# Splitting one store of a gated linear unit: tile 1's output as two transfers by rows

## The chip, the cores and the metric

The kernel runs on one core of a Trainium2 chip. The time is the device time of one execution in microseconds (us); the time before is the median of three runs, and lower is better. One more execution was recorded by the hardware profiler; its own time stands beside its span below.

## The reference

The input has 8192 rows of 8192 float32. The left half of each row is multiplied by the sigmoid of the right half, so the output has 8192 rows of 4096 float32.

```python
def reference(x):
    a, b = np.split(x, 2, axis=-1)
    return a * (1 / (1 + np.exp(-b)))
```

The kernel reads 268.44 MB and writes 134.22 MB.

## The kernel before

**Tiles.** The rows are cut into 33 tiles. Tiles 1 to 31 have 256 rows, two on each of the 128 partitions; tiles 0 and 32 have 128 rows, one on each partition. The two rows of a partition are neighbours in memory, so a partition of a full tile loads 64 KiB in one piece (two rows of 32 KiB) and stores 32 KiB in one piece (two rows of 16 KiB). There are two input buffers (`x_sb0`, `x_sb1`) and two output buffers (`o_sb0`, `o_sb1`); tile i uses number i % 2 of both.

**Engines.** For every tile SyncE issues the load (L46), ScalarE overwrites the right halves with their sigmoid (L59), VectorE multiplies into the output buffer (L73), and ScalarE issues the store (L83) on its own DMA queue; only the two stores of the last tile are issued by SyncE. In the profile, q1 is SyncE's queue (all loads and the last tile's stores), and q10 is ScalarE's (all other stores). Both queues feed the same 16 DMA engines. A full tile is worked on in one piece of 8192 elements per partition; tiles 1 and 31 in four of 2048, tile 0 in three pieces and tile 32 in two.

**What waits for what.** No scheduler is at work: the order is the program's.

- The load of tile i+2 waits until the multiplications of tile i have ended (semaphore `product`, L49), since they free the input buffer.
- The first sigmoid of a tile waits for its load. In tile 1, whose two rows per partition are loaded by two transfers, the third sigmoid waits for the second transfer (`row`, L68).
- The first multiplication of tile i waits on `ready[s]` both for its sigmoid and for the landing of the store of tile i-2, which frees the output buffer. `stored[s]` counts what such a store adds to that semaphore: 16 for each transfer.
- The store of tile i waits for `product` to reach `done[i]`, the number of multiplications up to and with tile i. It stands on ScalarE's queue behind the sigmoids of tile i and ahead of those of tile i+1. Tile 0 makes three products and tile 1 four, so `done[0]` is 3 and `done[1]` is 7.

The main loop is:

```python
for i in range(n):
    self.work(i, works.get(i, whole))
    if i + SLOTS < n:
        self.load(i + SLOTS)
    if i == 0:
        self.store(0, 0, half // 2, 2)
        self.store(0, half // 2, half, 3)
    elif i < n - 1:
        self.store(i)
```

`close` (L114 to L124) ends the program: SyncE waits for the last tile's stores, GpSimd for the other stores, and then clears the semaphores.

Of the kernel before, what the change touches and what calls it, by code (L numbers as in the profile page):

```python
# [16 lines left out]
class _Program:  # L17
# [75 lines left out]
    def trace(self):  # L93
        n, half = self.n_tiles, self.half
        one = slice(0, 1)
        whole = [(slice(0, R), slice(0, half))]
        fourths = [(slice(r, r + 1), c) for r in range(R) for c in HALVES]
        works = {0: [(one, c) for c in (QUARTERS[0], QUARTERS[1], HALVES[1])], 1: fourths,
                 n - 2: fourths, n - 1: [(one, c) for c in HALVES]}
        self.load(1, slice(0, 1))  # L100
        self.load(1, slice(1, 2), self.row)
# [4 lines that stand above are left out]
            if i == 0:  # L106
                self.store(0, 0, half // 2, 2)
                self.store(0, half // 2, half, 3)
            elif i < n - 1:
                self.store(i)  # L110
        for k, c in enumerate(HALVES):
            self.store(n - 1, c.start, c.stop, self.products - 1 + k)
# [69 lines left out]
```

## Time and profile before

| | |
|---|---|
| median of three runs | 933.2 us (933.19 to 933.42) |
| the profiled execution's own time | 933.03 us |
| its span | 931.7 us |
| DMA, mean over the span | 432 GB/s |
| VectorE busy | 279.1 us (30%) |
| ScalarE busy | 227.4 us (24%) |
| share of the DMA engines' time, q1 and q10 | 67.2% and 32.8% |

The span runs from the first to the last recorded instruction; the execution's own time is 1.3 us longer. The digits under "busy tenths" are shares of 40 equal slices of the span. A DMA "share" is the time that packets took, divided by 16 engines and by the stretch. A packet is what one DMA engine moves in one piece; the trace has a record of each with its start, its length and its size. Since a transfer of 128 partitions is spread over 16 engines, each engine has 8 of its packets, and behind them a packet of 4 bytes that counts up the semaphore. TensorE is not used.

### The profile page before, as it was taken

The numbers are of one execution on the slowest core, as the hardware profiler recorded it, in microseconds if no ns is written. First come the engines' busy times: TensorE is split into PE (matmuls) and PEld (weight loads), VectorE is DVE, ScalarE is ACT, GpSimd is POOL, SyncE is SP. The second block draws the span as 40 slices with busy tenths as digits, with TensorE's granted clock in tenths as the row PEclk, the third lists the DMA queues.
The fourth block names the chain that finished last, engine by engine and source line by source line (L and its number), as shares of the span: only waits on it lengthen the run. The fifth ranks groups of instructions, "written<-read, shape, count | busy, mean of one in ns | idle before, by whom it ended". The sixth has DMA issues, their size and how long they took to land.

```text
span 931.7 us, 200 instructions
## 1 busy us (share of the span) xinstructions
DVE 279.1 (30%) x42; ACT 227.4 (24%) x43; POOL 0.2 (0%) x4
## 2 busy tenths in 40 slices
DVE  1312333113332133321333213332133321333233
ACT  2332033320333202332023330233302333023331
POOL 0000000000000000000000000000000000000000
DMA  9999999999999999999999999999999999999999
GB/s 400 450 411 450 425 430 428 450 428 428 428 445 456 405 442 435 429 450 419 459 405 430 447 428 450 428 450 405 428 450 448 430 411 461 411 450 428 426 429 405
DMA packets 9937, 402.67 MB, mean 432 GB/s; under 512 B 1104, under 2 KB 1104, under 8 KB 1104
## 3 DMA queue, kind: packets, MB, share of 16 engines
q1 hardware_dynamic: 5184, 270.53, 67.2%
q10 hardware_dynamic: 4752, 132.12, 32.8%
q14 instruction: 1, 0.01, 0.0%
HBM read 268.44 MB, written 134.22 MB: 432 GB/s over the span
## 4 chain that ended last, share of the span: by engine, by line
DMA 73%; DVE 15%; ACT 12%; DVEq 0%; issue 0%
DMA x_sb<-in_x_dram 73%; DVE o_sb L73 15%; ACT x_sb L59 12%; DVEq L117 0%
## 5 line engine op out<-in xcount | busy, mean ns | idle before, releaser
L73 DVE TENSOR_TENSOR o_sb<-x_sb 128x8192 f32<-128x8192 f32 (+2 forms) x42 | 279.1, 6659 | 646.9 <-ACT x_sb L59 646.9
L59 ACT ACTIVATE x_sb<-x_sb 128x8192 f32<-128x8192 f32 (+2 forms) x42 | 226.1, 5401 | 694.5 <-DMA x_sb<-in_x_dram 694.5
L59 ACT ACT_TABLE_LOAD x1 | 1.3, 1283 | 1.5 <-PEq L148 1.5
L166 POOL MEMSET const-bfloat16-1.0<- 128x1 bf16 x1 | 0.1, 101 | 0.0
L166 POOL MEMSET const-uint8-127<- 128x1 uint8 x1 | 0.1, 101 | 0.0
L166 POOL MEMSET const-float32-0.0<- 128x1 f32 x1 | 0.1, 98 | 0.2 <-issue 0.2
L166 POOL MEMSET const-float32-1.0<- 128x1 f32 x1 | 0.1, 98 | 0.0
## 6 DMA issues: line engine op xcount, KB each, us to landing
out_dram<-o_sb ACTq DMA_DIRECT2D x31, 4096.0 KB, 34.8
x_sb<-in_x_dram SPq DMA_DIRECT2D x4, 4096.0 KB, 26.9
out_dram<-o_sb ACTq DMA_DIRECT2D x2, 1024.0 KB, 24.6
out_dram<-o_sb SPq DMA_DIRECT2D x2, 1024.0 KB, 5.5
x_sb<-in_x_dram SPq DMA_DIRECT2D x30, 42.2
```

The source lines that it names most:

```text
L59: sig = nc.scalar.activation(out=b, in_=b, func=mybir.ActivationFunctionType.Sigmoid)
L73: mul = nc.vector.tensor_mul(out=packed[:, r, c], in0=rows[:, r, 0, c], in1=rows[:, r, 1, c])
L166: nc = _bacc.Bacc("TRN2", target_bir_lowering=False, num_devices=1)
```

## The change

Tile 1's store was one transfer: 128 pieces of 32 KiB, issued when all four products of the tile were done. Now it is two transfers. The first takes the first row of every partition (128 pieces of 16 KiB) and waits for two products of tile 1, the second takes the second row and waits for all four. Both are issued by ScalarE one behind the other, where the one store was, and each adds 16 to `ready[1]`, for which the first multiplication of tile 3 waits. Nothing else differs.

```diff
             if i == 0:
                 self.store(0, 0, half // 2, 2)
                 self.store(0, half // 2, half, 3)
+            elif i == 1:
+                self.store(1, 0, half, self.done[0] + 2)
+                self.store(1, half, 2 * half, self.done[1])
             elif i < n - 1:
                 self.store(i)
```

## The prediction

> **What bounds the kernel now.** I read the page first: the span, the DMA slices, the queues.
>
> ```profile
> span 931.7 us, 200 instructions
> ...
> DMA  9999999999999999999999999999999999999999
> ...
> DMA packets 9937, 402.67 MB, mean 432 GB/s; under 512 B 1104, under 2 KB 1104, under 8 KB 1104
> ...
> q1 hardware_dynamic: 5184, 270.53, 67.2%
> q10 hardware_dynamic: 4752, 132.12, 32.8%
> ```
>
> The DMA engines are busy in every slice, and the two queues' shares add up to the whole span. The 1104 small packets are semaphore writes, 16 for each of 69 transfers. Busy time by stretch confirms it (columns: stretch, length, DVE, ACT, POOL, clock, DMA share, GB/s):
>
> ```profile
> 59.00:88.00 29.00, 8.69 (x1) 7.12 (x2) 0.00 (x0) 1.00 1.00 434
> 88.00:117.00 29.00, 8.69 (x1) 6.94 (x1) 0.00 (x0) 1.00 1.00 434
> ```
>
> A full tile takes 29.0 us of DMA and 15.7 us of engine work. Next the waits: engines wait for loads, and nothing waits for a store.
>
> ```profile
> ACT x_sb L59 <- DMA x_sb<-in_x_dram: 694.5, 34, 22.4
> DVE o_sb L73 <- ACT x_sb L59: 646.9, 35, 24.7
> ```
>
> Then the timeline around tile 1 and at the end (start, length, what):
>
> ```profile
> 41.48 0.36 ACTq L83 DMA_DIRECT2D out_dram<-o_sb  x1
> 59.07 7.03 ACT L59 ACTIVATE x_sb<-x_sb 128x8192 f32<-128x8192 f32 x1 [20.35 <-DMA x_sb<-in_x_dram]
> ...
> 87.91 7.03 ACT L59 ACTIVATE x_sb<-x_sb 128x8192 f32<-128x8192 f32 x1 [21.81 <-DMA x_sb<-in_x_dram]
> 94.97 8.69 DVE L73 TENSOR_TENSOR o_sb<-x_sb 128x8192 f32<-128x8192 f32 x1 [20.15 <-ACT x_sb L59]
> ```
> ```profile
> 919.57 3.71 ACT L59 ACTIVATE x_sb<-x_sb 128x2048 f32<-128x2048 f32 x2 [12.05 <-DMA x_sb<-in_x_dram]
> 921.51 4.49 DVE L73 TENSOR_TENSOR o_sb<-x_sb 128x2048 f32<-128x2048 f32 x2 [10.46 <-ACT x_sb L59]
> 923.83 3.02 SPq L83 DMA_DIRECT2D out_dram<-o_sb  x2
> ```
>
> Store 1 is issued at 41.48. The packet records place its first packet at 53.3, since the second store of tile 0 holds the queue until 50.6 (first engine) to 51.0. They also show the rule between the queues: each DMA engine alternates packet by packet, whatever the sizes: 64 KiB load, 8 KiB store, 64 KiB load at 34 to 50 us; 64 KiB, 32 KiB, 64 KiB afterwards. A semaphore write takes a turn too. So a full tile is 9 turns on either side, and loads and stores stay in step. Median packet times: 64 KiB 2.418 us, 32 KiB 1.213, 8 KiB 0.309, semaphore write 0.009.
>
> So the end is set by the sum of packet times, as long as neither queue's lag leaves the DMA engines without work.
>
> **The change part by part.**
>
> *More packets.* From 8 and 32 KiB, a packet is 37.7 ns per KiB plus 7.7 ns; 16 KiB gives 0.610 us. Each DMA engine has 16 x 0.610 in place of 8 x 1.213, and one more semaphore write: 8 x 7.7 + 9 = 70 ns. Successive packets overlap by some 4 ns in the records, so the lower bound is 0.03 us. I take +0.07 us: it lies on the bound resource.
>
> *The earlier first half.* Its two products end at 29.3, but ScalarE gets to it only behind the fourth sigmoid, at 38.7, still 2.8 us before 41.48. The queue ahead is full until 50.6, so no byte moves earlier: 0. Its issue takes 0.36 us on ScalarE, which is idle until 59: 0 as well. No load is behind it: those are on SyncE.
>
> *The turn count.* This is the real effect. Store 1 now takes 18 turns (16 packets, 2 semaphore writes) in place of 9, and loads get a 64 KiB packet against each 16 KiB. Counting from 53.3: 16 half packets (9.8 us) and the 15 load packets between them (36.3) put the second half's semaphore write at 99.3, where the single store's came at 79.9. Load 3 gains in the same turns: its last packet ends near 81, ScalarE starts at about 81.6 (before: 87.91). Its multiplication could start at 88.6 but now waits for store 1 until 99.8: a new wait of 11 us, end 108.5 (before 103.7). Behind it on VectorE nothing is due; ScalarE stands at store 3, so sigmoid 4 waits as well; SyncE's load 5 waits.
>
> Does DMA run dry? At 99.3 load 4 still has two packets and store 2 all eight: 2 x 2.42 + 8 x 1.21 = 14.5 us of work, until 113.8. Load 5 and store 3 are issued at 108.5. From issue to first packet I have 1.9 us as the upper value (final store: 923.83 to 925.74) and 1.05 as the lower (first load). So the queues fill again at 110.4, 3.4 us before the work ends. The load queue is empty from about 106.5, but DMA writes store 2 meanwhile, at the same 1.213 per packet as stores alone have at 919 to 925. Cost: 0, cover 3.4 us.
>
> *Afterwards.* Both sides are again 9 turns a tile, so the shift stays: loads land about 5 us earlier than before (tile 5's sigmoid near 141 instead of 146), stores land later, about 49 us after issue (now 34.8), and a multiplication may wait some us for its output buffer. Load i+2 is still issued more than 10 us before load i+1 ends.
>
> *The tail.* Before, the final stores' first packet at 925.74 follows directly the last of store 31 (925.73): no gap, no margin. After, load 32 lands about 5 us earlier, the final stores queue at about 921 and share turns with store 31. Order changes, the sum doesn't: 0.
>
> **Sum:** 933.03 + 0.07 = 933.10 for the profiled execution. The median of the runs is 0.17 above that execution, so +0.07 gives 933.27; I say 933.3. Bounds of the small terms: three stalls of some 0.35 us on load packets (at 18.6, at 50.5 when store 1 comes up, and one engine delayed at 718 by an instruction fetch, so that it ended 0.3 us behind the rest) may each go or come again: -0.8 to +0.8.
>
> [...] Two rows stand for what a further transfer costs: tile 0's two stores follow each other on the queue with only a load packet between, no gap; a final store, mostly uncovered, takes 5.4 us from issue to landing, of which 8 x 0.309 = 2.5 is movement. [...]
>
> **Rivals.**
>
> 1. *DMA runs dry once (slower).* If the alternation favours loads more than turn for turn, load 4 is finished before store 1 lands. Then store 2's 8 x 1.213 = 9.7 us must cover multiplication 3: 0.5 of landing, 8.7 and 1.9 make 11.1. Gap 1.4 us, and the first packet after an idle stretch took some 1.85 instead of 1.21: +2.0 in all, 935.1. It decides when less than 11.1 us of work is queued at store 1's landing; I count 14.5. It comes once, since load 5 and store 3 then start together. For it: the new wait on the chain. Against: the packet records alternate strictly from 34 to 60, at three packet sizes. Chance 0.09.
> 2. *The further transfer's fixed cost is paid (slower).* At most 5.4 - 2.5 = 2.9 us: 936.0. Against it the gapless stores of tile 0. Chance 0.04.
> 3. *The slack helps (faster).* The earlier loads relieve the tail and stalls vanish: 0.8 off, 932.4, still within 0.2%. Chance 0.08. More would need fewer packet times, and there is no idle DMA time to win: 0.03.
> 4. *The split doesn't shift the queues* (two 16 KiB pieces count as one turn): no wait appears, 933.2, same verdict. Chance 0.06.
>
> **How the numbers follow.** The forecast gets the remaining 0.70. Within 0.2% (1.9 us, about what a measurement of this kernel can tell from no change) lie the forecast, rival 4 and the smaller case of rival 3: 0.84. Slower: rivals 1 and 2, 0.13. Faster: 0.03. The range goes from the small terms' low end, 932.4, to rival 1's 935.1.
>
> **What would show it.** Right: 10081 packets, 1120 of them small; q10 4896; DMA share 1.00 in every 29 us stretch; tile 3's sigmoid near 81.6 and its multiplication near 99.8, put down to a store; stores landing about 49 us after issue. Rival 1 would show a stretch near 110 to 115 with a DMA share under 1. I am wrong if the tail shows idle DMA, or if tiles take more than 29.0 us each.

## The result, and the profile after

The change makes the kernel slower, by just under one per cent. Over 22 runs of each kernel the median is 941.84 us after and 933.06 before; the ratio, which goes by the means, is 1.0078, 95% interval 1.006 to 1.0095. The runs after fall into two groups: five between 933.17 and 933.66, as forecast, and seventeen between 940.57 and 944.68. The profiled execution is of the second group: 942.08 us, span 940.8.

The page after, the lines that answer to those shown of before:

```profile
span 940.8 us, 201 instructions
...
DMA  9999999999999999999999999999999999999996
GB/s 396 446 440 426 432 424 429 460 403 467 424 443 404 457 412 440 429 444 422 433 457 405 442 424 446 424 461 407 444 425 444 425 444 425 443 424 425 443 404 277
DMA packets 10081, 402.67 MB, mean 428 GB/s; under 512 B 1120, under 2 KB 1120, under 8 KB 1120
...
q1 hardware_dynamic: 5184, 270.53, 66.6%
q10 hardware_dynamic: 4896, 132.12, 32.6%
```

The packet counts are the forecast ones. DMA is busy throughout, except in the last slice. The timeline around tile 3 (start, length, what) is the forecast one too, to 0.5 us, up to the issue of store 3:

```profile
82.05 7.03 ACT L59 ACTIVATE x_sb<-x_sb 128x8192 f32<-128x8192 f32 x1 [17.15 <-DMA x_sb<-in_x_dram]
100.12 8.69 DVE L73 TENSOR_TENSOR o_sb<-x_sb 128x8192 f32<-128x8192 f32 x1 [26.50 <-DMA out_dram<-o_sb]
108.85 0.36 ACTq L83 DMA_DIRECT2D out_dram<-o_sb  x1
...
142.56 7.03 ACT L59 ACTIVATE x_sb<-x_sb 128x8192 f32<-128x8192 f32 x1 [26.28 <-DMA x_sb<-in_x_dram]
```

The time is lost later. From tile 5's sigmoid (142.56) to tile 31's (905.60) a tile takes (905.60 - 142.56) / 26 = 29.35 us instead of 29.0, although the windows show no idle DMA until near the end (stretch, length, DVE, ACT, POOL, clock, DMA share, GB/s):

```profile
860.00:889.00 29.00, 8.55 (x2) 7.03 (x1) 0.00 (x0) 1.00 1.00 434
889.00:918.00 29.00, 12.04 (x5) 7.31 (x4) 0.00 (x0) 1.00 0.97 417
918.00:931.00 13.00, 4.08 (x2) 3.71 (x2) 0.00 (x0) 1.00 0.75 321
931.00:940.80 9.80, 0.41 (x1) 0.00 (x0) 0.00 (x0) 1.00 0.45 186
```

The kernel before ended like this:

```profile
919.50:926.00 6.50, 4.49 (x2) 3.71 (x2) 0.00 (x0) 1.00 0.97 417
926.00:931.70 5.70, 0.00 (x1) 0.00 (x0) 0.00 (x0) 1.00 0.83 352
```

A share of 0.45 at the end means that some of the 16 DMA engines are done and others not. The packet records, put together into 16 sequences that have next to no gaps until 916 us, say which: 15 engines write their last packet between 935.1 and 935.3, one at 940.4. (The records do not name the engine. Where two engines change packets within a few ns the sorting is a choice; that moves single engines' figures below by up to about 1 us where all engines are stretched.) That one has 44 load packets stretched by 0.02 to 0.60 us between 118 and 905 us, in all 27 tiles from 5 to 31, 9.4 us together; the other 15 have none. Load 5's semaphore writes come at 140.4 to 140.9 from the 15 and at 142.2 from the one, load 31's at 894.4 to 895.0 and at 905.2; the sigmoids start at 142.56 and 905.60, so a tile waited for that engine's share of its load. From about 916 and 928 on the others run dry for 1.0 to 1.8 and about 2.5 us.

The same records give the one difference between that engine and the rest. Load 5's first packet starts at 112.6 to 113.1 on 15 engines, after seven packets of store 2. On the sixteenth it starts at 113.85, after all eight. Load 5 comes out of an empty queue (load 4's semaphore writes come at 106.5 to 107.0), and that engine took one more store first. Loads and stores both take 9 turns a tile in the records (8 packets and the semaphore write), and this difference of one turn is the same behind every store from 4 to 28.

I call the relation **lag**: how many turns an engine's stores run later against its loads than in the kernel before. The change leaves 15 engines at lag 5 and one at lag 4. It is read from the records by the load packet that follows a store's semaphore write.

### The profile page after: what moved, and what is told of

It is laid out like the page before. It is cut to its first block, busy times and chain, and to the rows that moved or that the text cites. A ratio compares the mean times of both kernels' runs of the same rounds, so it can differ in the third digit from the quotient of the medians.

```text
span 940.8 us, 201 instructions
## 1 busy us (share of the span) xinstructions
DVE 279.1 (30%) x42; ACT 227.4 (24%) x43; POOL 0.2 (0%) x4
## 4 chain that ended last, share of the span: by engine, by line
DMA 73%; DVE 14%; ACT 11%; DVEq 0%; issue 0%
DMA x_sb<-in_x_dram 68%; DVE o_sb L73 14%; ACT x_sb L59 11%; DMA out_dram<-o_sb 5%; DVEq L120 0%
## 6 DMA issues: line engine op xcount, KB each, us to landing
out_dram<-o_sb ACTq DMA_DIRECT2D x30, 4096.0 KB, 46.6
```

## The experiments

**First theory: out of step.** An engine that is a turn apart from the other 15 is disturbed by them. Rivals: the second transfer or the 16 KiB packets cost as such; the new wait of multiplication 3 costs.

*Two transfers by partitions.* (`store` gets an argument that picks the partitions.)

```diff
-                self.store(1, 0, half, self.done[0] + 2)
-                self.store(1, half, 2 * half, self.done[1])
+                self.store(1, parts=slice(0, 64))
+                self.store(1, parts=slice(64, 128))
```

> Store 1 goes as two transfers again, but of 64 partitions each with 32 KiB packets: 10 turns of the queue in place of 9, where the change has 18. Theory (out of step): no stretch with an empty load queue comes up, all 16 DMA engines stay in step, 933.1 us, at most 0.3 from it. Rival (a second transfer for tile 1 costs as such): about 941. Rival (the wait of multiplication 3 for its output buffer costs): no such wait here, 933.1.

Measured: 936.63 us, ratio 1.0038 (1.0026 to 1.005). The median engine has 2.5 us of stretched packets from 55 to 130 us, most on the second half's four store packets at 0.2 to 0.5 us each and 0.8 us on load 3's first packet, and none after. So the loss is local and not that of the change, but none of the three had priced it: cutting the store by partitions cost something of its own. The first half's packets lost only 0.2 us together; why the second half's lost more was not shown.

*Load 3 by rows as well.*

```diff
-            if i + SLOTS < n:
+            if i == 1:
+                self.load(3, slice(0, 1))
+                self.load(3, slice(1, 2))
+            elif i + SLOTS < n:
```

(The sigmoids of odd tiles from 3 on wait for 16 more on `loaded[1]`.)

> The change is kept, and load 3 is also cut by rows into two transfers of 32 KiB packets, so that loads and stores have 18 turns each. Theory (out of step): load 3 lands near 88 as before, multiplication 3 waits for no store, the load queue is never empty, no engine falls out of step: 933.2. Rival (16 KiB packets or the second transfer cost as such): about 941. Rival (the wait of multiplication 3 costs): 933.2.

Measured: 933.20 us, all eleven runs between 933.00 and 933.77, ratio 1.0001 (0.9993 to 1.001). All engines have lag 0. Tile 3's sigmoid starts at 88.30, its multiplication at 95.36 behind ScalarE. The split and its 16 KiB packets cost nothing that these runs can tell when the turns stay balanced.

*Load 5 later by 0.8 and by 1.2 us.* Ahead of tile 3's multiplication its first 600 (960) elements are multiplied once more:

```diff
         for (r, c), wait in zip(pieces, waits):
+            if i == 3:
+                head = slice(0, 600)
+                extra = nc.vector.tensor_mul(out=packed[:, 0, head], in0=rows[:, 0, 0, head], in1=rows[:, 0, 1, head])
+                extra._wait_ge(*wait)
+                extra.then_inc(self.product, 1)
+                self.products += 1
+                wait = (self.product, self.products)
```

> The change is kept; ahead of the multiplication of tile 3 VectorE multiplies its first 600 elements once more, so load 5 is issued some 0.8 us later (about 109.7 instead of 108.85). Theory (out of step): load 5's packets then arrive near 112.1, between the packet boundaries of the 16 engines (111.25 to 111.74 and 112.46 to 112.95 in the profile of the change), all engines take the same turn, and the time is about 933.2 in all or nearly all runs although a delay was added. Rival (the wait of multiplication 3 moves the chain): 942 to 943, not under the change's 941.8. Rival (half rows or a second transfer cost as such): 941 to 943.

> As the kernel with 600 repeated elements, but with 960, so load 5 is issued some 1.2 us later than in the change: one 32 KiB packet. Theory (out of step): its packets arrive near 112.5, within the next group of packet boundaries (112.46 to 112.95), the engines part again, and most runs take 940 to 945. Rival (delay as such helps, or it is chance): 933 as the shorter delay. Rival (the wait moves the chain): 942 to 943.

Measured: 951.42 us (1.0196, 1.0182 to 1.0209) and 959.64 (1.0279, 1.0247 to 1.031). Both miss, and the first one fells the theory. In its profile all 16 engines start load 5 between 113.8 and 114.2, after all eight packets of store 2, so they are in step, and all 16 have lag 4; each has 10.7 to 17.7 us of stretched load packets from 155 to 900 us. DMA is counted as busy all that time and moves less (before, then the kernel with 600 repeated elements):

```profile
490.00:780.00 290.00, 86.92 (x10) 70.29 (x10) 0.00 (x0) 1.00 1.00 434
```
```profile
490.00:780.00 290.00, 84.78 (x10) 70.29 (x10) 0.00 (x0) 1.00 1.00 424
```

**Second theory: lag.** The lag itself decides, engine by engine. To set it without the stretch of an empty load queue, store 1 is cut into one large and n small transfers, which gives 9 + n turns:

```diff
+                self.store(1, parts=slice(0, 64))          # n = 4
+                for p in range(64, 128, 16):
+                    self.store(1, parts=slice(p, p + 16))
```

> Store 1 is cut by partitions into one transfer of 64 and four of 16, all of 32 KiB packets: 13 turns in place of 9, so the store queue falls 4 turns behind the load queue without any stretch with an empty load queue and without a wait of a multiplication. New theory (lag): a DMA engine is slowed on load packets in every tile when its stores run 4 turns later against its loads than before, as all 16 engines did in the kernel with 600 repeated elements. Then some 10 us and more of stalls on load packets after 120 us on every engine, 943 to 953. Rival (the stalls come from the stretch with an empty load queue, or from engines that are apart): none here, only the local cost of cut stores (3.5 us for two halves of 64 partitions): 934 to 938.

> As the one of 13 turns, with 14: one transfer of 48 partitions and five of 16, 5 turns later than before. That is the lag of the 15 undisturbed engines in the profile of the change. Theory (lag): no stalls per tile, only the local cost of the cut store: 934 to 938. Rival (more small transfers cost more): above the kernel of 13 turns. Rival (empty load queue): 934 to 938 as well.

> 12 turns (80 partitions and three times 16): 3 turns later. Theory (lag) has no measured row for 3; it says that the time is either 934 to 938, with no stalls per tile, or over 940 with stalls in every tile, and that this falls together in each run. Rival (empty load queue): 934 to 938.

> 11 turns (96 partitions and twice 16): 2 turns later. Theory (lag): as for 3 turns, no row yet; 1 turn later gave no stalls per tile. Rival (empty load queue): 934 to 938.

> Store 1 in 15 turns (one transfer of 32 partitions, six of 16): 6 turns later than before. So far 0, 1, 2 and 5 turns gave no stalls in later tiles, 3 and 4 did, and five engines at 6 turns in the kernel with 600 products less had none either. Theory (lag): no stalls after tile 6, only the local cost of the cut store, 936 to 941. Rival (more small transfers cost more): over 942.

The table puts them beside the others. "Stretch" is the excess of load packets over 2.418 us on the median engine (lowest to highest) from 155 to 900 us; "local" is the median excess of all packets at 55 to 130 us, the price of the cut itself. Times are medians of 2 to 22 runs; lag, stretch and local come from the one profiled execution of each kernel, which lies within 2 us of the median except with 960 elements repeated (951.15 us; the other five runs took 958.6 to 963.6 and have no trace).

| kernel | lag | time, us | stretch, us | local, us |
|---|---|---|---|---|
| before | 0 | 933.06 | 0 (0 to 0.24) | 0 |
| load 3 by rows as well | 0 | 933.20 | 0 (0 to 0.25) | 0 |
| two transfers by partitions | 1 | 936.63 | 0 (0 to 0.25) | 2.5 |
| 11 turns | 2 | 939.64 | 0 (0 to 0.24) | 4.1 |
| 12 turns | 3 | 972.06 | 26.4 (24.4 to 29.0) | 6.0 |
| 13 turns | 4 | 961.41 | 18.5 (16.4 to 20.2) | 6.2 |
| 600 elements repeated | 4 | 951.42 | 15.1 (10.7 to 17.7) | 0.2 |
| 960 elements repeated | 4 | 959.64 | 14.4 (12.8 to 17.4) | 0.1 |
| the change | 5, one engine 4 | 941.84 | 0, that engine 8.6 | 0 |
| 14 turns | 5 | 937.92 | 0 (0 to 0.25) | 3.0 |
| 15 turns | 6 | 939.43 | 0 | 3.6 |

In these profiles the median engine's loads were stretched at lags 3 and 4 (14.4 to 26.4 us) and not at lags 0, 1, 2, 5 and 6 (0). 12 and 14 turns differ by two small transfers, and the one with more of them is 34 us faster. Two expectations were missed in size: 13 turns came out above 943 to 953, and 11 turns between the two ranges that were named, because the local cost had been put at 3.5 us and was up to 9.9 us on one engine. In the kernels of 11, 14 and 15 turns the local cost (6.6, 5.2 and 5.9 us on the worst engine) makes up nearly all of the distance from 933.1. At 12 turns nothing waits for a store; the windows and the waits of that kernel:

```profile
490.00:780.00 290.00, 86.93 (x10) 64.62 (x10) 0.00 (x0) 1.00 1.00 418
```
```profile
ACT x_sb L59 <- DMA x_sb<-in_x_dram: 729.8, 34, 28.0
DVE o_sb L73 <- ACT x_sb L59: 682.2, 35, 26.3
```

*Load 5 earlier by 0.6 us.*

```diff
+            if i == 3:
+                c = slice(0, 3796)
             mul = nc.vector.tensor_mul(
```

> The change, with tile 3's multiplication cut from 4096 to 3796 elements in each row (600 products per partition are left out of the output), so load 5 is issued some 0.6 us earlier: the opposite of the kernel with 600 repeated elements. Theory (lag): in the change load 5's packets arrive just as the 16 engines choose between a store and a load packet; earlier by 0.6 us all of them take load 5 one turn sooner, all have a lag of 5 turns, no stalls in later tiles, and every run takes about 933.2. Rival (the wait of multiplication 3, or the stretch with an empty load queue, costs as such): 941 as the change.

Measured: 933.22 us, ratio 1.001 (0.9994 to 1.0026) without the three slowest of twelve runs. Eight of twelve runs lie at 932.97 to 933.24, four at 940.8 to 963.1, so "every run" was too much. Three of the four, at 954 to 963 us, are slower than any run of the change, and with them the mean is 940.2; none of the four was profiled, so which lags they had is not known (lag 7 was not tried). The profile is of the first kind and speaks against two rivals. Five engines have lag 6 and eleven lag 5: apart, and not stretched. And this is its span and its waits:

```profile
span 931.9 us, 201 instructions
```
```profile
ACT x_sb L59 <- DMA x_sb<-in_x_dram: 670.2, 33, 25.6
DVE o_sb L75 <- DMA out_dram<-o_sb: 585.2, 29, 26.5
```

29 multiplications wait for their output buffer, and the kernel is as quick as the one before: a wait on the chain cost nothing here, with a DMA share of 1.00 at 434 GB/s from 200 to 780 us.

**What collides at lag 3.** Three edits to the kernel of 12 turns, one at a time: compute of tiles 4 to 31 cut to 64 elements; output buffers exchanged; loads of tiles 4 to 31 from the addresses of tiles 4 and 5.

```diff
+        works.update({i: [(one, slice(0, 64))] for i in range(4, n - 1)})
```
```diff
+        self.os = self.os[::-1]
```
```diff
-in_=self.x[i][:, part])
+in_=self.x[4 + i % 2 if 4 <= i < self.n_tiles - 1 else i][:, part])
```

> The kernel of 12 turns (lag 3, 972 us), with sigmoid and multiplication of tiles 4 to 31 cut to 64 elements per partition (the rest of these tiles' work is left out). Theory A (the two streams disturb each other inside the DMA path): the stalls stay, 965 to 975. Theory B (DMA meets ScalarE's and VectorE's accesses to the buffers): the stalls after tile 4 go, 938 to 944.

> The kernel of 12 turns (lag 3), with the two output buffers exchanged, so that a load and the store that it meets in its DMA engine stand at other distances inside a partition. Theory S (packets collide by their places in the buffers): the time changes, to under 950 if the distance decides. Theory H (collide in memory outside, or in the engine itself): 968 to 976 as before.

> The kernel of 12 turns (lag 3), in which the loads of tiles 4 to 31 all read the addresses of input tile 4 or 5 (the output is that of these tiles), so that distances between what is read and what is written differ in every tile. Theory H (packets collide by their addresses in memory outside): the stalls change a lot, time under 960 or above 985. Theory S (places in the buffers) or the engine itself: 968 to 976 as before.

Measured, two runs each: 975.26, 974.35 and 974.87 us (ratios 1.0452, 1.0442, 1.0448, each within 0.0018); median stretches 28.6, 27.3 and 29.7 us. None of the three edits took the stretch away: not the cut compute, not the exchanged buffers, not the other addresses read. Then the stores' source:

```diff
-        ins = queue.dma_start(out=self.out[i][parts, lo:hi], in_=self.os[s][parts, lo:hi])
+        source = self.x[i] if 4 <= i < self.n_tiles - 1 else self.os[s]
+        ins = queue.dma_start(out=self.out[i][parts, lo:hi], in_=source[parts, lo:hi])
```

> The kernel of 12 turns (lag 3, 972 us), in which the stores of tiles 4 to 31 copy the same number of bytes from the input in memory to the output instead of from the output buffers (the products of these tiles are left out of the output). Theory P (a store's read and a load's write meet in the same partition of the on-chip memory): the stalls on load packets after tile 4 go, under 945. Theory E (the engine's two queues disturb each other by their order alone, or reading and writing memory outside does): the stalls stay, over 960.

Measured: 947.60 us in two runs, ratio 1.0154 (1.0134 to 1.0175): over the expected 945, with all engines still at lag 3, but the stretch is gone (0, at most 0.24), and what is left is the local cost of the cut (7.7 us on the median engine, up to 10.1) and tiles 4 and 5, whose loads still met stores from the buffers. The windows are back at the rate of before:

```profile
490.00:780.00 290.00, 86.93 (x10) 70.31 (x10) 0.00 (x0) 1.00 1.00 434
```

So at lag 3 loads were stretched beside stores that read the output buffers (26.4 us) and not beside stores that read the input in memory (0). The order of one engine's packets shows where loads and stores stand to each other (l and s for load and store, tile and number of the packet in its tile, between 405 and 430 us):

```
lag 0  l15.0 s13.3 l15.1 s13.4 l15.2 s13.5
lag 3  l15.0 s13.0 l15.1 s13.1 l15.2 s13.2
lag 4  l15.1 s13.0 l15.2 s13.1 l15.3 s13.2
lag 5  l15.2 s13.0 l15.3 s13.1 l15.4 s13.2
```

At lag 3 a store packet follows directly the load packet of the same number; at lag 4 it comes one load later. Why loads were stretched in these two orders was not shown. Theory P's place for it, a partition common to both, was a guess: the traces do not show partitions, and no kernel moved the partitions against the turns. Why lag 2, where the store packet comes directly before the load of the same number, had no stretch (0) also stays open.

**Two controls on the change itself.** The split at tile 15, and both halves of store 1 issued late:

```diff
+            elif i == 15:
+                self.store(15, 0, half)
+                self.store(15, half, 2 * half)
```
```diff
-                self.store(1, 0, half, self.done[0] + 2)
+                self.store(1, 0, half)
```

> The change made at tile 15 in place of tile 1 (both halves wait for all four quarters' worth of products, that is for the tile's only multiplication). Theory (lag, a cost in every later tile): the same arrival decides for load 19, and where one engine gets lag 4 it loses some 0.33 us in each of the 13 or 14 tiles left instead of 28: 933.2 in the undisturbed runs, 936 to 938.5 in the others. Rival (a cost paid once at the cut): 941 to 945 as in the change.

> The change with both halves issued after the fourth product, at 41.5, so that nothing is issued early. Both theories: the queue is full until 50.6 anyway, so nothing moves; 933.2 in some runs and 940 to 945 in most, as the change. If the earlier issue mattered, it would be either all 933 or over 946.

At tile 15: median 934.65 us over ten runs (1.0019, 1.0007 to 1.0032), five at 933.1 to 933.8 and five at 935.5 to 938.0. In the profile two engines have lag 4 and lose 3.0 and 4.4 us in the tiles left, the others nothing. The cost is paid in the later tiles: 9.4 us in the 27 tiles of the change, 3.0 and 4.4 in the 13 or 14 left here. With both halves late: median 938.45 over ten runs, from 932.9 to 948.4, four of them at 932.9 to 934.1 and five over 941 (ratio 1.0056, 1.0023 to 1.0089). That is neither all 933 nor over 946, though "most" at 940 to 945 was too much; the earlier issue has no part that these runs can tell. Its profile caught an execution in which all 16 engines got lag 5, which is the change as forecast: span, and the landing of stores and loads (count, KB each, median us).

```profile
span 931.9 us, 201 instructions
...
out_dram<-o_sb ACTq DMA_DIRECT2D x30, 4096.0 KB, 49.2
...
x_sb<-in_x_dram SPq DMA_DIRECT2D x30, 42.1
```

## Why the prediction was wrong

**Right: the turn count.** Forecast and profile: sigmoid 3 at 81.6 and 82.05, multiplication 3 at 99.8 and 100.12, load 5 issued at 108.5 and 108.84, tile 5's sigmoid near 141 and at 141.38 (lag 5 everywhere) or 142.56, stores landing after 49 and 49.2 us (lag 5 everywhere) or 46.6. DMA never ran dry there, as said (next to no gaps in the records until 916 us), so rival 1 did not happen; nor did rival 4. The earlier issue was worth nothing, as said, though it came sooner than said: not behind the fourth sigmoid at 38.7 but beside the third, into a store queue that was full all the same (store 1's first packets start at 53.0 to 53.5).

```profile
35.16 1.91 ACT L59 ACTIVATE x_sb<-x_sb 128x2048 f32<-128x2048 f32 x1 [8.43 <-DMA x_sb<-in_x_dram]
35.17 0.34 ACTq L83 DMA_DIRECT2D out_dram<-o_sb  x1
```

**Right: the price of the split itself.** 0.07 us was forecast, too little for these runs to tell; with turns balanced the measured ratio is 1.0001 (0.9993 to 1.001), and a 16 KiB packet took 0.611 us (forecast 0.610). Rival 2, the fixed cost of one more transfer (2.9 us), falls with the same run. Rival 3, a gain, did not show either: the fastest of the 22 runs took 933.17 us.

**Wrong: "So the end is set by the sum of packet times", with each time taken as a constant.** The table of packet times came from one relation of the two queues, the one that the kernel before happens to hold, and I carried it over to another ("Both sides are again 9 turns a tile, so the shift stays"). The shift did stay, and that is where the loss is: a load packet takes 2.418 us at lags 0 and 5, and up to 0.6 more on the engine at lag 4, 9.4 us in all. Both signs of being wrong that the prediction names came: 29.35 us a tile, and idle DMA in the tail. The warning was the sentence itself: a lasting new relation of two streams, of which the trace held no row. It should have had bounds; I gave it none.

**Wrong: how soon load 5 joins.** The sum took at most 1.9 us from issue to first packet and so a cover of 3.4 us. The first packets came 3.8 to 5.0 us after the issue, when 15 engines had one store packet left and the sixteenth had none:

```profile
108.84 0.33 SPq L46 DMA_DIRECT2D x_sb<-in_x_dram  x1
```

The trace of before had a nearer row than the two that were used, a transfer that enters an empty queue while the other queue is full: tile 0's first store, whose first packet starts at 20.17, 4.5 us after its issue (both figures include the wait for the packet under way).

```profile
15.64 3.04 ACTq L83 DMA_DIRECT2D out_dram<-o_sb  x2
```

The missing cover cost nothing by itself, but this arrival is what set the lag: 0.8 us later all 16 engines had lag 4, 0.6 us earlier eleven had 5 and five 6.

**Wrong: one representative engine.** I counted the turns of one DMA engine, and load 5's arrival decides between lag 5 and lag 4 on each of 16. In the profile 15 have the lag at which the forecast times come out. One that chose a packet later was enough, because tiles waited for its share (semaphore write at 905.2, sigmoid 31 at 905.60). That the engines are some 0.4 us apart (load 5's first packets start at 117.32 to 117.74) was in the trace of before and not in the sum. But this spread alone does not decide: engines that ended a packet at 112.60 and 112.65 took load 5, and the one that did so at 112.64 took the store. Whether load 5 reached the engines at different moments as well, the records do not show. That five runs of 22 are as forecast and seventeen are not fits a choice that falls anew in each run, but of these 22 only one was profiled.

**Wrong: the range.** Its upper end was rival 1's single gap. No rival had a cost that recurs in every later tile, the kind that added 9 us here.

## What to carry to other kernels

In this kernel the two DMA queues share the engines and kept them busy (67.2% and 32.8% of their time before). Their order was the same from tile to tile, and an edit that shifted one against the other was paid, or not, in the later tiles (26.4 us at lag 3, 0 at lag 5): look at how long single packets take in the new order and not at the busy share, which was 1.00 at 434 GB/s and at 418. When one transfer is cut, keep the number of turns equal on both queues (cut the partner too: 933.20). And where a queue is let run empty, look at the turn at which each engine takes up its refill: here 15 did after seven store packets and one after eight, and that one ended at 940.4 us, the others by 935.3.

## What the runs showed of the hardware that was not expected

- A DMA engine's 64 KiB load packets (2.418 us) were stretched when its stores from the output buffers stood 3 or 4 turns later than in the kernel before: by up to 0.6 us on the one engine of the change, by up to 1.1 us where all engines are at lag 3 or 4. That made 26.4 us a kernel at lag 3, 14 to 19 at lag 4, 0 at the other five lags tried. With stores that read the input in memory instead (lag 3): 0.
- With store 1 cut by partitions packets were stretched at 55 to 130 us: 2.5 us for two halves, up to 9.9 us on one engine for 80 + 3 x 16 partitions.
- Engines within 0.5 us of each other served different queues next at load 5, not in the order of their times; the lags that came of it (5 and 4) then lasted for 800 us.
- A load issued into an empty queue beside a full store queue had its first packet 3.8 to 5.0 us after issue in the profile of the change, against 1.05 to 1.5 us for the first load of the kernel.
